# A fixed engine order for the first norm and its products, whole-tile squares, small constants on two other queues, and S5's small steps behind the norm

## The chip, the core and the metric

The kernel runs on one core of a Trainium2 chip. Its engines each work through their own instructions in order: PE (TensorE, matmuls), DVE (VectorE), ACT (ScalarE), POOL (GpSimd) and SP, which here issues DMAs. ACT and POOL can issue DMAs too. The metric is device microseconds (us) of one execution; lower is better.

## The reference

A two-layer trunk on 256 latent and 256 context tokens of 1024 features. Each sub-layer is an RMSNorm, a shift and scale from a conditioning vector (adaLN), the sub-layer itself, and a gated residual. Layer 0 is a half SwiGLU feed-forward of 2816 hidden features, a mixer (latent attention beside an S5 state space), and another half feed-forward. The place of this study is the first feed-forward and what runs beside it:

```python
def rmsnorm(x, g):
    xf = x.astype(jnp.float32)
    y = xf * lax.rsqrt(jnp.mean(xf * xf, axis=-1, keepdims=True) + NORM_EPS)
    return (y * g.astype(jnp.float32)).astype(x.dtype)

def adaln_params(cond, w, b):
    m = jax.nn.silu(cond) @ w + b
    return m.reshape(cond.shape[0], 1, N_MOD, D_MODEL)

def ffn_half_step(h, m, k, g, w_gate, w_up, w_down):
    shift, scale, gate = m[:, :, 3 * k], m[:, :, 3 * k + 1], m[:, :, 3 * k + 2]
    hn = modulate(rmsnorm(h, g), shift, scale)
    return h + 0.5 * gate * swiglu(hn, w_gate, w_up, w_down)

def s5_discretise(lam_re, lam_im, log_step, b_re, b_im):
    ...
    step = jnp.exp(log_step.astype(f32))[:, None]
    a_bar = jnp.exp(lam * step)
    b = lax.complex(b_re.astype(f32), b_im.astype(f32))
    b_bar = ((a_bar - 1.0) / lam)[..., None] * b
    return a_bar, b_bar
```

## The kernel before, in words

**Data.** The activations `res` lie transposed in SBUF, 128 features by 8 tiles by 512 tokens (context first). Weights come in 512 KB blocks of 128 x 1024. A product in fp32 is made of three matmuls of high and low parts, wh·xh, wh·xl and wl·xh (L160 to L162 in `mm3`); the high part of a weight block is a cast on ACT (L150), the low part a subtraction on DVE (L151), both in `wload`. There are four buffers for blocks as loaded (`raw`), four for blocks as split (`w`), and six PSUM banks (`mm`) for products, two more (`ps`) for other things.

**Start (`build`).** SP loads `res`, the conditioning vectors `ct`, S5's parameters, then the first layer's first two modulation vectors' weights `modw0` in sixteen blocks of 512 KB with the first four feed-forward blocks between them, and the small constants `sel`, `ident`, `modb`, `gain`, `sig` behind the first two blocks. The squares for the norm are taken for each tile and each half of the tokens (ACT) and summed on DVE (L297, L298).

**First norm and its products (`norm_proj` with `lead`).** `mod_first(i)` makes shift and scale of tile i: eight matmuls (L191), a copy (L200), two products with `sel` (L203), and small fixes on DVE (`mod_fix`, L177 to L182). `rstd_steps` takes the mean of squares by PE (L255) and the reciprocal root on DVE in three iterations (L266 to L275), `rstd_rows` spreads it over the partitions (L284). `norm_tile` makes tile i's normed input: L315 on DVE, the high part on ACT (L320), the low part on DVE (L322). Four weight blocks are multiplied tile by tile into four banks; I call this the lead.

**Then the feed-forward (`ffn`).** The hidden features come in three chunks of 6, 8 and 8 blocks. For every block: silu (L470), times up (L471), split (L166, L167). After a chunk, `down` makes eight products of 18 (later 24) matmuls, and each leaves its bank through `residual` (L435), which multiplies by the gate. Beside this run background jobs, moved on by `tick` at given rates: S5's preparation (`s5_prepare` with `s5_small`, 128x64 steps on DVE, then `s5_chunk`) and the other modulation vectors (`mod_job`): each is eight 512 KB loads into two buffers `m` and sixteen reduces on DVE (L227). The gate of the first feed-forward, mod(0,2), is the first vector of `mod_job`.

**Order.** A scheduler lays out each engine's order when the program is built, from the order in which the code is written, from priorities (`high_priority`) and from its estimate of when each input is ready; on the chip each engine then runs its list as it stands.

Of the kernel before, what the change touches and what calls it, by code (L numbers as in the profile page):

```python
# [13 lines left out]
ALU = mybir.AluOpType  # L14
# [50 lines left out]

class Builder:
# [180 lines left out]
    def rstd_steps(self, accs, inv, more=None):  # L247
# [17 lines left out]
        def steps():  # L265
# [5 lines left out]
            for _ in range(3):  # L271
                for c in cs:
# [33 lines left out]
    def norm_tile(self, l, k, i, h, x, keep=True):  # L306
# [14 lines left out]
        return lambda: self.keep(  # L321
            nc.vector.scalar_tensor_tensor(x[:, 1, c0:c1], y, b, x[:, 0, c0:c1], op0=ALU.add, op1=ALU.subtract)  # L322
        )

    def norm_proj(self, l, k, halves, srcs, lead=None, spare=None):
# [4 lines left out]
        if lead is not None:  # L330
            ws = self.w0
            first = self.tc.high_priority
            pss = [self.pm() for _ in srcs]
            with first(offset=SOON):
                mods = [lead(i) for i in range(KT)]
                st = self.rstd_stats([self.acc[h] for h in halves], self.inv_d)
                next(mods[0])
                rb = self.rstd_rows(*st)
                for h in halves:
                    self.rb[h] = rb[:, h[0] : h[1]]  # L340
            for i in range(KT):
                with first(offset=SOON):
                    if i + 1 < KT:
                        next(mods[i + 1])
                    next(mods[i], None)
                    for low in [self.norm_tile(l, k, i, h, xs[i]) for h in halves]:
                        low()
                for w, ps in zip(ws, pss):
                    self.mm3(ps, self.wparts(w, KT)[i : i + 1], self.parts(xs[i : i + 1], 0, T2), i == 0, i == KT - 1)
# [40 lines left out]
        return xs, pss  # L390

# [159 lines left out]
    def s5_small(self):  # L551
# [7 lines left out]
        nc.sync.dma_start(bank[1][:, 0:3, :], t["s5_par"])  # L559
# [24 lines left out]
        expm1(step, lst)  # L584
# [61 lines left out]
        yield  # L646
# [489 lines left out]
    def lru_decay(self):  # L1136
# [6 lines left out]
        v.scalar_tensor_tensor(z, lam, -1.0, lam, op0=ALU.mult, op1=ALU.min)  # L1143
# [216 lines left out]
    def build(self):  # L1360
# [220 lines left out]
```

## Time and profile before

| | us |
|---|---|
| runs, three | 1765.08, 1766.74, 1766.30 |
| median | 1766.3 |
| the profiled execution | 1764.04 |
| its span | 1762.0 |
| PE busy | 1702.8 (97%) |
| DVE busy | 1267.6 (72%) |
| ACT busy | 693.7 (39%) |

The profile is of one execution, whose time is 2.0 us more than the span from its first to its last instruction. A busy share over the whole span hides what happens in a stretch; the change touches the first 130 us, and the rows below are from there, with one place near 1520 us that shows PE behind an idle. In the timeline each row is the start, the time, the engine, the line, the operation, output and inputs, and a count; a bracket tells how long the engine was idle before and what ended that.

### The profile page before, as it was taken

To read this page: it belongs to the slowest core of one execution; us is meant where nothing else is said; L and a number is where in the kernel's file an instruction comes from. 1 tells how busy PE (TensorE), PEld (TensorE's weight loads), DVE (VectorE), ACT (ScalarE), POOL (GpSimd) and SP (SyncE) were. 2 spreads that over 40 slices of the span, in tenths; PEclk is the share of its full clock that TensorE was granted. 3 is DMA by queue.
4 is the path that set the end of the run, shared out by engine and by line. 5 is a ranking of instruction groups with operands and counts; after the bars stand their busy time and mean duration, and the time that the engine had idled before them with its cause. 6 is when DMAs were issued, how large, how long until landed. Compare 5 with 4: busy or idle time off the path is not lost.

```text
span 1762.0 us, 24867 instructions
## 1 busy us (share of the span) xinstructions
PE 1702.8 (97%) x9380; PEld 1443.5 (82%) x9380; DVE 1267.6 (72%) x2545; ACT 693.7 (39%) x1101; POOL 13.2 (1%) x47
## 2 busy tenths in 40 slices
PE   5999999999989999999999999999999999699998
PEld 3788878889878788778888888888888888499998
DVE  7999999987488668776676686555543576976675
ACT  4433333443445654222222233222222357554443
POOL 0000000000000000000000000000000000000000
PEclk9999999999998999999999999999999999899999
DMA  9566767662465453564554443555533225155552
GB/s 330 172 221 213 228 212 229 215 189 95 126 188 166 132 188 107 171 216 147 164 190 157 159 141 124 181 185 155 169 120 96 96 96 187 67 171 189 183 183 90
DMA packets 107480, 292.65 MB, mean 166 GB/s; under 512 B 21152, under 2 KB 35360, under 8 KB 107104
## 3 DMA queue, kind: packets, MB, share of 16 engines
q1 hardware_dynamic: 101504, 286.86, 50.6%
q10 hardware_dynamic: 5216, 2.62, 0.8%
q0 software_dynamic: 640, 1.57, 0.3%
q8 instruction: 74, 1.21, 0.3%
q14 instruction: 46, 0.38, 0.1%
HBM read 272.20 MB, written 18.28 MB: 165 GB/s over the span
## 4 chain that ended last, share of the span: by engine, by line
PE 89%; DVE 6%; DMA 2%; issue 1%; SPq 1%; ACT 1%; DVEq 0%; ACTq 0%
PE mm L160 25%; PE mm L162 25%; PE mm L161 25%; PE mm L157 7%; DVE w L151 1%; DMA h<-in_modw_dram 1%; PE mm L1207 1%; SPq L1040 1%; DMA x<-d_g 1%; PE mm L907 1%; DVE x L322 0%; DVE nt L315 0%; PE mm L191 0%; PE ps L690 0%; PE ps L1118 0%
## 5 line engine op out<-in xcount | busy, mean ns | idle before, releaser
L150 ACT CAST w<-raw 128x1024 fp32r<-128x1024 f32 (+2 forms) x324 | 328.8, 1019 | 530.6 <-PE mm L162 262.2
L161 PE MATMUL mm<-x,w 128*128 128x512 f32 (+1 forms) x1424 | 519.8, 365 | 0.0
L162 PE MATMUL mm<-x,w 128*128 128x512 f32 (+1 forms) x1424 | 519.2, 365 | 0.0
L160 PE MATMUL mm<-x,w 128*128 128x512 f32 (+1 forms) x1424 | 514.6, 367 | 3.5 <-ACT x L320 2.2
L151 DVE TENSOR_TENSOR w<-raw,w 128x1024 fp32r<-128x1024 f32 (+2 forms) x324 | 383.8, 1186 | 150.5 <-ACT w L150 149.3
L160 PEld LDWEIGHTS mm<-x,w 128*128 128x128 f32 x1424 | 267.4, 189 | 49.5 <-ACT x L320 2.5
L161 PEld LDWEIGHTS mm<-x,w 128*128 128x128 f32 x1424 | 268.6, 189 | 43.8 <-issue 2.0
L162 PEld LDWEIGHTS mm<-x,w 128*128 128x128 f32 x1424 | 268.5, 189 | 43.9 <-issue 1.2
L227 DVE CUSTOM_DVE_ANT_0 junk<-m,sc 128x1024 f32<-128x1024 f32 x224 | 273.0, 1219 | 1.8 <-DMA m<-in_modw_dram 0.4
L160 PE MATMUL mm<-h,w 128*128 128x512 f32 x456 | 178.3, 394 | 0.0
L162 PE MATMUL mm<-h,w 128*128 128x512 f32 x456 | 176.9, 390 | 0.0
L161 PE MATMUL mm<-h,w 128*128 128x512 f32 x456 | 176.7, 390 | 0.0
L435 DVE SCALAR_TENSOR_TENSOR res<-mm,mraw,res 128x256 f32<-128x256 f32 x192 | 86.0, 479 | 96.5 <-PE mm L162 87.2
L471 DVE TENSOR_TENSOR h<-h,mm 128x512 f32<-128x512 f32 x66 | 45.3, 686 | 108.1 <-PE mm L162 95.8
L470 ACT ACTIVATE h<-mm 128x512 f32<-128x512 f32 x66 | 39.5, 598 | 196.0 <-PE mm L162 185.2
L160 PEld LDWEIGHTS mm<-h,w 128*128 128x128 f32 x456 | 85.6, 188 | 18.9 <-issue 1.1
L162 PEld LDWEIGHTS mm<-h,w 128*128 128x128 f32 x456 | 85.6, 188 | 18.5 <-issue 0.6
L161 PEld LDWEIGHTS mm<-h,w 128*128 128x128 f32 x456 | 85.6, 188 | 18.4 <-issue 1.0
L160 PE MATMUL mm<-hy,w 128*128 128x258 f32 x352 | 99.2, 284 | 0.7 <-DVE g L499 0.7
L162 PE MATMUL mm<-hy,w 128*128 128x258 f32 x352 | 99.6, 283 | 0.0
L161 PE MATMUL mm<-hy,w 128*128 128x258 f32 x352 | 99.6, 283 | 0.0
L157 PE MATMUL mm<-x,w 128*128 128x256 f32 x384 | 66.3, 290 | 6.7 <-DVE x L322 6.2
(371 smaller groups left out, 2002.1 us busy)
## 6 DMA issues: line engine op xcount, KB each, us to landing
raw<-in_wgu_dram SPq DMA_DIRECT2D x176, 512.0 KB, 3.9
m<-in_modw_dram SPq DMA_DIRECT2D x130, 512.0 KB, 4.3
raw<-in_wd_dram SPq DMA_DIRECT2D x64, 512.0 KB, 3.6
raw<-in_wd_dram SPq DMA_DIRECT2D x32, 384.0 KB, 3.3
raw<-in_od_in_dram SPq DMA_DIRECT2D x20, 512.0 KB, 3.5
h<-in_modw_dram SPq DMA_DIRECT2D x12, 512.0 KB, 10.0
raw<-in_ev_in_dram SPq DMA_DIRECT2D x10, 512.0 KB, 3.5
d_mb<-mbt SPq DMA_DIRECT2D x16, 256.0 KB, 3.4
```

What stands on the lines that cost most here:

```text
L150: nc.scalar.copy(hi[:, :n], raw[:, :n])
L151: nc.vector.tensor_sub(lo[:, :n], raw[:, :n], hi[:, :n])
L157: mm = lambda *a, **k: self.keep(self.nc.tensor.matmul(*a, **k))
L160: mm(ps, lhsT=wh, rhs=xh, start=first and i == 0, stop=False)
L161: mm(ps, lhsT=wh, rhs=xl, start=False, stop=False)
L162: r = mm(ps, lhsT=wl, rhs=xh, start=False, stop=last and i == n - 1)
L227: nc.vector.tensor_tensor_reduce(self.junk, w, self.sc[:, v, :], 1.0, 0.0, ALU.mult, ALU.add, raw[:, dt, v : v + 1])
L435: self.nc.vector.scalar_tensor_tensor(r, ps[:, c0:c1], gate[:, i, VEC[h] : VEC[h] + 1], r, op0=ALU.mult, op1=ALU.add)
L470: nc.scalar.activation(s[:, 0, lo:hi], pg[:, lo:hi], AF.Silu)
L471: nc.vector.tensor_mul(s[:, 1, lo:hi], s[:, 0, lo:hi], pu[:, lo:hi])
L907: nc.tensor.matmul(ps, lhsT=q[0:96, c : c + P], rhs=k[0:96, :nk], start=True, stop=True)
L1040: nc.sync.dma_start(uy[g * 16 : (g + 1) * 16, 1, :].rearrange("p (s n) -> p s n", s=L), d_y[i * 8 + g].rearrange("s c n -> c s n"))
```

## The change

1. PE, DVE and ACT instructions of the first norm and its four products are tied, each to the one before it on its engine, so that the scheduler keeps the order in which `lead_products` is written. Its order: modulation of tile 0, statistics, two weight casts, root, rows, norm of tile 0 with the two low weight parts between; then for each tile the four products, with the next tile's norm behind the first product and the modulation of the tile after that ahead of the fourth. In the listing of the changed kernel these instructions all stand at L74, the wrapper's call.
2. The squares are taken of whole tiles of 128x512, into buffers of S5 that are not yet in use; the last tile's squares are added by PE. The root's iterations work on 128x4 at once.
3. `ct`, `modb` and `gain` are loaded by ACT's queue, `sel`, `ident`, `sig` and S5's parameters by POOL's.
4. S5's first exponential and `lru_decay`'s first step are put behind the lead's last low part; S5's small part yields eight times at its end instead of once.

```diff
+class InOrder:
...
+    def __getattr__(self, name):
+        def call(*a, **k):
+            ins = getattr(self.eng, name)(*a, **k)
+            if self.last is not None:
+                dep = mybir.DependencyInfo(mybir.DependencyClass.NoSync, mybir.DependencyReason.DATA)
+                self.tc.add_manual_dep(ins.ins, self.last, dep, reason="in order")
+            self.last = ins.ins.name
+            return ins
...
+                if n == 4:
+                    k(dv.tensor_mul(a, y, y))
+                    k(dv.tensor_mul(a, a, v))
+                    k(dv.scalar_tensor_tensor(y, a, 1.5, y, op0=ALU.add, op1=ALU.mult))
...
+    def lead_products(self, l, k, halves, xs, pss, mods):
...
+        next(mods[0])
+        rb, y = self.rstd_stats(*self.first_sums)
+        ws = [cast(r) for r in self.w0[:2]]
+        next(mods[0], None)
+        rb = self.rstd_rows(rb, y)
...
+        lows = norm(0)
+        ws[0][1]()
+        for low in lows:
+            low()
+        ws[1][1]()
+        next(mods[1])
+        ws += [cast(r) for r in self.w0[2:]]
+        for i in range(KT):
+            product(0, i)
+            if i + 1 < KT:
+                next(mods[i + 1], None)
+                lows = norm(i + 1)
+                if i == 0:
+                    ws[2][1]()
+                for low in lows:
+                    low()
+                if i == 0:
+                    ws[3][1]()
+            product(1, i)
+            product(2, i)
+            if i + 2 < KT:
+                next(mods[i + 2])
+            product(3, i)
...
-        nc.sync.dma_start(bank[1][:, 0:3, :], t["s5_par"])
+        nc.gpsimd.dma_start(bank[1][:, 0:3, :], t["s5_par"])
...
-        expm1(step, lst)
+        with self.tc.issue_after(self.last_low.ins):
+            expm1(step, lst)
...
-        yield
+        for _ in range(8):
+            yield
...
+            sq = [self.slot("mb", [P, T2]), self.slot("mbt", [P, T2]), et[:, 0], et[:, 1]]
+            acc = self.slot("bank", [P, 912])[:, :T2]
             for i in range(KT):
-                for h in both:
-                    self.stat(i, h)
+                A.activation(sq[i % 4] if i else acc, self.res[:, i], AF.Square)
+                if 0 < i < KT - 1:
+                    V.tensor_add(acc, acc, sq[i % 4])
+            self.first_sums = [acc], self.inv_d, sq[(KT - 1) % 4]
```

In the changed kernel the lines move: the weight's low part is L180, products L189 to L191, reduces L256, the eviction L508, S5's small matmuls L785.

**The order on PE at the start.** Before (mm_68 to mm_71 are the four products' banks, mm_77 and mm_79 the modulation of tiles 0 and 1):

```order
L191 MATMUL mm_77_332<-h_21_175,ct_18_127 32x256 x4
L191 MATMUL mm_77_332<-h_22_176,ct_18_127 32x256 x4
L255 MATMUL ps_73_297<-inv_d_169,acc_44_236 128x1 x2
L255 MATMUL ps_73_297<-inv_d_169,acc_45_238 128x1 x2
L203 MATMUL mm_77_332<-sel_179,nt_78_341 128x2 x2
L191 MATMUL mm_79_347<-h_27_199,ct_18_127 32x256 x4
L191 MATMUL mm_79_347<-h_28_200,ct_18_127 32x256 x4
L203 MATMUL mm_79_347<-sel_179,nt_80_356 128x2 x2
L284 MATMUL ps_72_296<-ident_181,rs_y_75_303 128x128 x4
L160 MATMUL mm_68_292<-x_60_284,w_24_191 128x512
```

and now (mm_52 and mm_53 are the first two of the four products' banks, mm_56 and mm_67 the modulation of tiles 0 and 1, bank and et the sums of squares):

```order
L74 MATMUL mm_56_256<-h_21_184,ct_18_127 32x256 x4
L74 MATMUL mm_56_256<-h_22_185,ct_18_127 32x256 x4
L74 MATMUL ps_59_268<-inv_d_133,bank_43_227 128x1
L74 MATMUL ps_59_268<-inv_d_133,et_40_224 128x1
...
L74 MATMUL ps_59_268<-inv_d_133,et_40_224 128x1
L74 MATMUL mm_56_256<-sel_139,nt_57_265 128x2 x2
L74 MATMUL ps_58_267<-ident_141,rs_y_61_278 128x128 x4
L74 MATMUL mm_67_315<-h_25_192,ct_18_127 32x256 x4
L74 MATMUL mm_67_315<-h_26_193,ct_18_127 32x256 x4
L74 MATMUL mm_52_252<-x_44_244,w_63_292 128x512 x3
L74 MATMUL mm_67_315<-sel_139,nt_68_324 128x2 x2
L74 MATMUL mm_53_253<-x_44_244,w_64_294 128x512 x3
```

The statistics matmuls are twice as many, the rows (`ident`) have moved ahead of the modulation of tile 1, and each weight block's three matmuls now stand together.

**The order on DVE beside the norm.** Before, around the low part of tile 1 (x_61 is its normed input, sb0 and sb1 hold S5's small values):

```order
L322 SCALAR_TENSOR_TENSOR x_61_285<-nt_85_399,mraw0_0_282,x_61_285 128x256
L580 TENSOR_TENSOR sb1_20_163<-sb1_20_163 128x64
L322 SCALAR_TENSOR_TENSOR x_61_285<-nt_86_402,mraw0_0_282,x_61_285 128x256
L582 TENSOR_TENSOR sb1_20_163<-sb1_20_163 128x64
L591 TENSOR_TENSOR sb1_20_163<-sb1_20_163 128x64
L604 TENSOR_TENSOR sb0_19_162<-sb1_20_163 128x64
L622 TENSOR_TENSOR s5_rho_726<-sb1_20_163 128x64
L613 TENSOR_TENSOR sb1_20_163<-sb0_19_162,sb1_20_163 128x64
L177 TENSOR_TENSOR mraw0_0_282<-mm_83_383,modb_183 128x2
L177 TENSOR_TENSOR mraw0_1_283<-mm_83_383,modb_183 128x2
L598 TENSOR_TENSOR sb1_20_163<-sb1_20_163 128x64
L616 TENSOR_TENSOR sb0_19_162<-sb0_19_162,sb1_20_163 128x64
```

and now, the last tile's low parts and what stands behind them:

```order
L74 SCALAR_TENSOR_TENSOR x_51_251<-nt_95_556,mraw0_0_242,x_51_251 128x256
L74 SCALAR_TENSOR_TENSOR x_51_251<-nt_96_559,mraw0_0_242,x_51_251 128x256
L640 TENSOR_SCALAR sb1_20_182<-sb1_20_182 128x64
L610 TENSOR_SCALAR sb1_20_182<-sb1_20_182 128x64
L611 TENSOR_SCALAR sb1_20_182<-sb1_20_182 128x64
L615 TENSOR_SCALAR sb1_20_182<-sb1_20_182 128x64
L616 TENSOR_TENSOR sb1_20_182<-sb1_20_182 128x64
L615 TENSOR_SCALAR sb1_20_182<-sb1_20_182 128x64
```

S5's small steps stood among the norm's; now all but five of them follow the last low part, and the first hidden block's L544 among them.

**The order on DVE at the first down product.** Before, from the last of the gate's reduces on (mraw0_2 is the gate mod(0,2); mm_204, mm_211 and so on are the down products' banks; w_241, w_248, w_256 weight blocks):

```order
L227 ISA junk_110_625,mraw0_2_819<-m_148_998,sc_109_624 128x1024
L227 ISA mraw0_2_819 128x1
L730 TENSOR_TENSOR et_177_1193<-et_177_1193,sb0_19_162 128x8x4
L686 TENSOR_TENSOR mb_159_1078<-mb_159_1078,tm_145_979 128x512
L151 TENSOR_TENSOR w_248_1668<-raw_247_1666,w_248_1668 128x768
L177 TENSOR_TENSOR mraw0_2_819<-mraw0_2_819,modb_183 128x16
L701 TENSOR_TENSOR tm_145_979<-pb_114_749,bank_144_977 128x576
L182 TENSOR_SCALAR mraw0_2_819<-mraw0_2_819 128x16
L702 TENSOR_TENSOR gs_162_1090<-gs_162_1090,tm_145_979 128x576
L435 SCALAR_TENSOR_TENSOR res_75<-mm_204_1354,mraw0_2_819,res_75 128x256 x2
L435 SCALAR_TENSOR_TENSOR res_75<-mm_211_1414,mraw0_2_819,res_75 128x256 x2
L435 SCALAR_TENSOR_TENSOR res_75<-mm_219_1466,mraw0_2_819,res_75 128x256 x2
```

and now, from the split of w_247 to the first evictions (mm_182 and mm_189 are the first two down products; the rows left out are seven more of the gate's reduces, each with its second row, and S5's steps):

```order
L180 TENSOR_TENSOR w_247_1711<-raw_246_1709,w_247_1711 128x1024
L256 ISA junk_98_586,mraw0_2_763<-m_108_782,sc_97_585 128x1024
L256 ISA mraw0_2_763 128x1
...
L256 ISA junk_98_586,mraw0_2_763<-m_128_901,sc_97_585 128x1024
L256 ISA mraw0_2_763 128x1
L206 TENSOR_TENSOR mraw0_2_763<-mraw0_2_763,modb_143 128x16
L256 ISA junk_98_586,mraw0_3_1014<-m_142_1015,sc_97_585 128x1024
L256 ISA mraw0_3_1014 128x1
L211 TENSOR_SCALAR mraw0_2_763<-mraw0_2_763 128x16
L508 SCALAR_TENSOR_TENSOR res_75<-mm_182_1268,mraw0_2_763,res_75 128x256 x2
L508 SCALAR_TENSOR_TENSOR res_75<-mm_189_1315,mraw0_2_763,res_75 128x256 x2
```

The gate's reduces had all run ahead of the seventh and eighth down products' weight splits; now nine of sixteen stand behind the split of w_247, a block for the next chunk, and the evictions behind them.

**PE at the same place**, now (mm_220 is the sixth down product, mm_229 the seventh, which takes the bank of mm_182):

```order
L191 MATMUL mm_220_1523<-h_152_1090,w_219_1520 128x512
L189 MATMUL mm_220_1523<-h_172_1209,w_219_1520 128x512
L190 MATMUL mm_220_1523<-h_172_1209,w_219_1520 128x512
L191 MATMUL mm_220_1523<-h_172_1209,w_219_1520 128x512
L785 MATMUL ps_139_983<-gs_137_973,bank_119_860 32x128 x4
L785 MATMUL ps_139_983<-gs_138_978,bank_119_860 32x128 x4
L189 MATMUL mm_229_1574<-h_100_592,w_228_1571 128x512
```

Between the two products PE has only two groups of S5's matmuls.

## Rows read from the trace of the kernel before

**Rows 1.** The page, part 1: busy time, share of the span, instructions.
```profile
PE 1702.8 (97%) x9380; PEld 1443.5 (82%) x9380; DVE 1267.6 (72%) x2545; ACT 693.7 (39%) x1101; POOL 13.2 (1%) x47
```
**Rows 2.** Stretches: length, busy PE, PEld, DVE, ACT, POOL, then clock, DMA share, GB/s.
```profile
28.20:35.00 6.80, 6.80 (x44) 3.62 (x45) 6.66 (x40) 2.06 (x6) 0.00 (x0) 1.00 1.03 411
62.00:126.00 64.00, 63.60 (x296) 51.54 (x297) 61.31 (x120) 24.63 (x39) 0.11 (x1) 1.00 0.63 199
```
**Rows 3.** The timeline of the front: start, time, engine, line, operation.
```profile
14.74 1.87 PE L255 MATMUL ps<-inv_d,acc 128*128 128x1 f32 x8
...
16.64 0.16 DVE L266 TENSOR_SCALAR rs_v<-ps 128x4 f32<-128x4 f32 x1 [0.54 <-PE ps L255]
...
22.52 0.35 DVE L275 SCALAR_TENSOR_TENSOR rs_y<-rs_a,rs_y 128x1 f32<-128x1 f32 x4
...
23.97 2.05 PE L284 MATMUL ps<-ident,rs_y 128*128 128x128 f32 x8
...
25.43 1.22 DVE L151 TENSOR_TENSOR w<-raw,w 128x1024 fp32r<-128x1024 f32 x1
...
26.74 0.86 DVE L315 SCALAR_TENSOR_TENSOR nt<-res,mraw,ps 128x256 f32<-128x256 f32 x2
...
28.20 2.08 PE L160 MATMUL mm<-x,w 128*128 128x512 f32 x4 [2.18 <-ACT x L320]
...
61.11 0.39 PE L162 MATMUL mm<-x,w 128*128 128x512 f32 x1
...
62.19 0.19 PEld L160 LDWEIGHTS mm<-x,w 128*128 128x128 f32 x1 [1.12 <-ACT w L150]
```
**Rows 4.** The timeline of the first down product, the same columns.
```profile
118.44 0.39 PE L162 MATMUL mm<-h,w 128*128 128x512 f32 x1
...
118.60 1.22 DVE L227 CUSTOM_DVE_ANT_0 junk<-m,sc 128x1024 f32<-128x1024 f32 x1
118.67 0.39 PE L160 MATMUL mm<-h,w 128*128 128x512 f32 x1
...
119.74 0.08 DVE L227 DVE_READ_ACCUMULATOR2_ANT mraw<- 128x1 f32 x1
...
125.57 3.22 DVE L435 SCALAR_TENSOR_TENSOR res<-mm,mraw,res 128x256 f32<-128x256 f32 x8
...
134.68 1.05 ACT L150 CAST w<-raw 128x1024 fp32r<-128x1024 f32 x1 [3.63 <-PE mm L162]
```
**Rows 5.** The chain of waits from 0 to 90 us: start, time, step.
```profile
35.38 0.34 PE mm L203 x4
...
39.07 1.86 PE mm L191 x32
```
**Rows 6.** DMA issues: queue, count, KB each, median us to landing.
```profile
m<-in_modw_dram SPq DMA_DIRECT2D x130, 512.0 KB, 4.3
...
d_y<-ys POOLq DMA_DIRECT2D x8, 128.0 KB, 2.9
```
**Rows 7.** Groups on DVE, 0 to 58.1 us: busy time, mean ns, idle before.
```profile
L577 DVE TENSOR_TENSOR sb<-sb 128x64 f32<-128x64 f32 x12 | 2.6, 214 | 0.1
```
**Rows 8.** Groups on DVE by shape, 62 to 126 us, the same columns.
```profile
L700 DVE TENSOR_TENSOR gs<-pa,bank 128x576 f32<-128x576 f32 x4 | 2.8, 751 | 0.0
...
L684 DVE TENSOR_TENSOR mb<-pa,bank 128x512 f32<-128x512 f32 x4 | 2.7, 683 | 0.0
...
L730 DVE TENSOR_TENSOR et<-et,sb 128x128 f32<-128x128 f32 x1 | 0.3, 284 | 0.0
```
**Rows 9.** Tile m, 60 to 140 us: its loads, from issue to landing.
```profile
DMA to landing us min/median/max: 3.5/4.2/4.6
```
**Rows 10.** The timeline of PE near 1520 us.
```profile
1520.18 8.86 PE L1311 MATMUL mm<-hy,x 128*128 128x256 f32 x32 [6.24 <-DVE x L1296]
```
**Rows 11.** Stretches behind that idle, columns as in rows 2.
```profile
1520.20:1523.60 3.40, 3.40 (x8) 2.78 (x9) 3.40 (x6) 0.63 (x1) 0.00 (x0) 0.50 0.00 0
1523.60:1526.00 2.40, 2.40 (x12) 2.12 (x12) 2.40 (x5) 0.00 (x0) 0.00 (x0) 1.00 0.00 0
```

More of the change, by code (lines that the diff above doesn't have):

```diff
@@ L63, with __init__, __getattr__ @@
 LN_PARTS = _split3(math.log(2.0), 9, 11)
+class InOrder:
+    def __init__(self, tc, eng):
+        self.tc, self.eng, self.last = tc, eng, None
+    def __getattr__(self, name):
[6 more added lines that the diff above has]
+            return ins
+        return call
+class InOrderCore:
+    def __init__(self, tc, nc):
+        self.nc = nc
+        self.tensor, self.vector, self.scalar = (InOrder(tc, e) for e in (nc.tensor, nc.vector, nc.scalar))
+    def __getattr__(self, name):
+        return getattr(self.nc, name)
 class Builder:
@@ L330, in norm_proj @@
         if lead is not None:
-            ws = self.w0
-            first = self.tc.high_priority
             pss = [self.pm() for _ in srcs]
[L334 to L349, printed above, removed]
+            with self.tc.high_priority(offset=SOON):
+                self.nc = self.core
+                self.lead_products(l, k, halves, xs, pss, [lead(i) for i in range(KT)])
+                self.nc = self.tc.nc
             return xs, pss
@@ L390, in norm_proj, with cast, norm, product @@
         return xs, pss
+    def lead_products(self, l, k, halves, xs, pss, mods):
+        nc = self.nc
+        def cast(raw):
+            w = self.wp.tile([P, 2, 1024], F32R, tag="w", name=self.uid("w"))
+            nc.scalar.copy(w[:, 0], raw)
+            return w, lambda: nc.vector.tensor_sub(w[:, 1], raw, w[:, 0])
+        def norm(i):
+            return [self.norm_tile(l, k, i, h, xs[i]) for h in halves]
+        def product(b, i):
+            w = ws[b][0]
+            self.mm3(pss[b], self.wparts((w[:, 0], w[:, 1]), KT)[i : i + 1], self.parts(xs[i : i + 1], 0, T2), i == 0, i == KT - 1)
+        next(mods[0])
[3 more added lines that the diff above has]
+        rb = self.rstd_rows(rb, y)
+        for h in halves:
+            self.rb[h] = rb[:, h[0] : h[1]]
+        lows = norm(0)
[21 more added lines that the diff above has]
+            product(3, i)
     def parts(self, xs, c0, c1):
@@ L1380, in build @@
         self.inv_d, self.inv_q, self.inv_kv = invs
-        small = lambda: [
-            setattr(self, nm, self.const(shape, nm, t[nm]))
-            for nm, shape in (("sel", [P, 2]), ("ident", [P, P]), ("modb", [P, 2, 9, KT]), ("gain", [P, 7, KT]), ("sig", [P, 3]))
-        ]
+        for nm, shape, q in (
+            ("sel", [P, 2], nc.gpsimd),
+            ("ident", [P, P], nc.gpsimd),
+            ("modb", [P, 2, 9, KT], nc.scalar),
+            ("gain", [P, 7, KT], nc.scalar),
+            ("sig", [P, 3], nc.gpsimd),
+        ):
+            setattr(self, nm, self.const(shape, nm, t[nm], queue=q))
+        s5 = self.s5_prepare()
+        next(s5)
         self.mw0, self.w0 = [], []
```

34 lines of the change are left out of this document (20 added, 14 removed).

## The prediction

> **What bounds the kernel now.** I read the page first, then the stretches, then the front and the first down product in the timeline. TensorE is busy 97% of the span [rows 1], and from 62 to 126 us for 63.60 of 64.00 us; DVE is busy for 61.31 of the same 64, and for 6.66 of 6.80 us where the products begin [rows 2]. So PE sets the time, and behind it DVE has hardly a gap for the first 130 us: work put later on DVE comes out later at its end.
>
> The front, in order [rows 3]: the eight statistics matmuls take 1.87 us from 14.74, the rsqrt chain on DVE runs from 16.64 to 22.87 (22.52 + 0.35), the rows are spread by PE from 23.97, a weight's low part is taken at 25.43, the first norm at 26.74, the first product begins at 28.20. The lead's last matmul starts at 61.11 (and PE is free of it near 61.35); the next weight load stands 1.12 us idle and comes at 62.19.
>
> The second place is the first down product. Its result leaves PSUM only through L435, which wants the gate mod(0,2); this comes out of sixteen reduces on DVE, each 1.22 us long, 1.14 from its start to the next instruction (118.60 to 119.74) [rows 4]. The gate was done just ahead of 125.57, where eight evictions run in 3.22 us; the sixth down product's weight buffer came free at 134.68, where ACT casts the next block into it [rows 4]. Six banks hold six down products; the seventh needs the first one's bank. In this run that bank was free some 8 us before PE wanted it: 134.68 against 125.57 + 0.8 for the first bank's two evictions (3.22 / 8 x 2). That margin is what this change is about.
>
> **The change part by part.** *The front.* Whole-tile squares whose last tile PE adds make sixteen statistics matmuls of eight: +1.87, at the same price. The rsqrt chain of 6.23 us had splits and S5 rows among its own; in program order it is 3 steps and 3 times 3 dependent instructions on 128x4, 12 in all. A row of this kind lasts 0.16 [rows 3]; with the hand-over between dependent ones I take 0.24, between 0.16 and 0.35 (the last step before): 2.9, so -3.3. The rows no longer stand behind tile 1's modulation matmuls: 23.97 against 22.87, -1.1. No split stands between rows and first norm: 25.43 to 26.65, of which 0.7 lay beside the rows' matmuls, so about -0.7 (bounds 0 and -1.2). Tile 1's modulation matmuls now stand ahead of the first product: +0.7 (0.93 a tile, half of 1.86 [rows 5], less what lies beside the norm). First loads are issued a little earlier: -1 (0 to -1.5). Sum: 1.87 - 3.3 - 1.1 - 0.7 + 0.7 - 1 = -3.5, first product at about 24.7.
>
> Half of that is given back. All four low parts were taken before the first product or just at it; now two of them, and the norm of tile 1, stand inside the first round. From the first norm on, about 23.4, DVE owes four splits at 1.13 (1.22 less what laps over), two tiles of norm and low parts at 0.86 a pair [rows 3] and small fixes: 4.5 + 3.4 + 0.6 = 8.5, so the fourth product of tile 0 ends near 32. Behind it PE owes 28 products of three matmuls, 84 x 0.23 (118.44 to 118.67 [rows 4]) = 19.2, five tiles' modulations at 0.93, six times L203 at 0.34 [rows 5], and about 1.9 for changes of form and a late load: 27.8. The lead ends near 59.7, where it ended at 61.35: -1.7; the pause behind it shrinks by 0.5. **Front: -2.2**, bounds 0 (all given back) and -5.
>
> *Constants on other queues.* They are issued sooner and land in a few us: POOL's transfers landed in 2.9 us, the modulation blocks on SP in 4.3 [rows 6]. I take nothing beyond the 1 us above. The Trainium skill, "SBUF - State Buffer" (the warning on the "DVE blocks DMA" trap in its part on the two sides of SBUF), speaks against POOL's queue: its descriptors are written by GpSimd, which certain DVE instructions lock out. No row here shows such a lock: POOL's eight transfers of one kind landed in 2.9 us, within 1.5 us of SP's. What it would do is the third rival.
>
> *S5 behind the last low part.* Some 140 small S5 rows of 128x64 ran among the norm's before; a row lasts 0.21 [rows 7], 0.13 from start to start. Now all but five come after the lead: 140 x 0.13 = 18 us of DVE, moved from a stretch where PE waited for DVE little to one where DVE is full. In the order, the gate's reduces stand behind them: only one of the sixteen stands ahead of the sixth down product's weight split, and between the split of w_247 and the second eviction of mm_182 stand eleven reduces (nine of the gate, two of mod(0,3)). This split is the trap: w_247 goes into the buffer of w_219, the sixth down product's weights, so its cast waits until PE has finished that product. PE then wants the seventh, mm_229, whose bank is mm_182's. So PE stands, from the end of the sixth down product, for:
> cast 1.05 [rows 4]; split 1.13; eleven reduces x 1.14 = 12.5; nineteen S5 and gate rows between them, two of 128x576 at 0.75, one of 128x512 at 0.68, six of 128x128 at 0.28 [rows 8], ten smaller at a mean of 0.28, 6.7 in durations, less 0.08 each for lapping = 5.2; two evictions 0.8. Together 20.7. The modulation blocks have two buffers; a block lands 3.5 to 4.6 us after issue [rows 9], and two reduces with the rows beside them fill about 3.1, so three blocks come 0.5 to 1.4 late: +2. Signals between engines +0.5. **Stall: 23** (21 to 27).
>
> PE comes out of it at half clock. Behind a 6.24 us idle, ended at 1520.18 [rows 10], the granted clock was 0.50 for the 3.4 us to 1523.6, then 1.00 [rows 11]: level 1.2 instead of 2.4 GHz, so half of 3.4 is lost: **+1.7**.
>
> *Is any of it hidden or won back?* PE is the bound, so a stall of PE is time unless later work of PE is waiting on something else. S5's transposes that PE had done by then before are now done later: the same work, neither sum changes. DVE stays 12 to 18 us of work behind and loses no slack it needs, since later evictions do not wait for a modulation: 0, bounds -3 and +5.
>
> Sum: -2.2 + 23 + 1.7 = +22.5 on the profiled execution's 1764.0 (span 1762.0 and 2.0 around it) = 1786.5. The median of the three runs, 1766.3, is 2.3 above the profiled one: 1788.8, **1789 us**.
>
> **The rivals.** *Short stall (1770 to 1781).* DVE, which takes its rows in order, is ahead of what I count: if w_247's cast gets its buffer sooner or reduces overlap the wait, only part of the eleven stands in PE's way. For it: DVE's rows ahead of w_247 have some waits that I could only sum. Against: the buffer chain above is fixed by the order. +4 to +15. Chance 0.06.
>
> *No stall: the change does what it is written to do (1760 to 1766).* The gate's reduces would have to be done within the 8 us margin; it decides whether S5's rows ahead of the first eviction cost DVE less than 8 us more than before. For it: the front frees DVE of some 3 us. Against: 18 us moved. Then only the front's 0 to -5 is left, 1764 in the middle. This is the faster side. Chance 0.08.
>
> *The constants come late.* By the rule above the transfers of `sel` and `ident` would wait for DVE: the chain that needs them ends on DVE at about 19 to 20, and a landing of 2.9 us from there puts the row matmuls 3 to 4 us later, eats the front's gain and leaves the stall: 1789 + 3 = 1792, up to 1794. For it: DVE is full there. Against: DVE waits for the statistics just before (0.54 [rows 3]), and the transfers are issued before DVE's first sum. Chance 0.04.
>
> *DVE stays the bound through the first feed-forward (1797 to 1816).* After the stall DVE has the same backlog; if silu products and splits are then late chunk after chunk, another 10 to 25 us come on top. For it: DVE's 61.31 of 64.00. Against: PE was busy 63.60 of the same 64 [rows 2], so a full DVE alone did not hold it. Chance 0.05.
>
> *The order does nothing:* front as before, no stall, 1765 to 1769. Chance 0.02.
>
> **How the numbers follow.** Forecast 0.75 (1782 to 1797 by its own bounds), the others 0.06, 0.08, 0.04, 0.05, 0.02. The range 1779 to 1798 holds the forecast, late constants, and an edge of the short stall and of the bound DVE: about 0.81. About 0.2%, 3.5 us, is what a measurement of this kernel can tell from no change: faster 0.05 (the larger half of the case without a stall), same 0.06 (the rest of it, the order that does nothing, and a stall of a few us), slower 0.89.
>
> **What would show it.** One idle of 20 to 27 us on PE near 130 us, ahead of mm_229's first matmul, ended by the eviction L508; clock 0.50 behind it; eleven L256 reduces inside; the first product at 24 to 25.5 and the lead's end at 59 to 61. If that idle is under 15 us, or PE's idle comes elsewhere, the step on the gate's place is wrong; if the first product starts later than 28, the front is.

## The result, and the profile after

The changed kernel took 1788.87 us (median of 4 runs, 1788.55 to 1789.97), the kernel before beside it 1765.69 (4 runs): 1.0135 of it, 95% interval 1.0122 to 1.0148, 23.2 us slower. The span of the profiled execution grew from 1762.0 to 1786.8.

The page of the changed kernel, part 1, to be held beside [rows 1]: PE and DVE are as busy as before in microseconds, so nearly all of the 24.8 us is waiting.

```profile
PE 1704.7 (95%) x9388; PEld 1444.8 (81%) x9388; DVE 1271.4 (71%) x2492; ACT 692.6 (39%) x1092; POOL 15.4 (1%) x51
```

What PE waited for in its first 200 us, in the changed kernel (total, times, longest):

```profile
PE mm L189 <- DVE res L508: 21.6, 1, 21.6
...
PE ps L785 <- DVE gs L777: 1.5, 1, 1.5
...
PE mm L74 <- DVE w L74: 1.3, 1, 1.3
```

One wait of 21.6 us on an eviction. The timeline of the changed kernel around it, DVE, ACT and PE together (compare [rows 4]):

```profile
130.35 1.04 ACT L179 CAST w<-raw 128x1024 fp32r<-128x1024 f32 x1 [1.46 <-PE mm L191]
...
132.01 1.22 DVE L180 TENSOR_TENSOR w<-raw,w 128x1024 fp32r<-128x1024 f32 x1
132.15 0.43 PE L785 MATMUL ps<-gs,bank 128*32 128x128 f32 x8 [1.48 <-DVE gs L777]
...
133.15 1.22 DVE L256 CUSTOM_DVE_ANT_0 junk<-m,sc 128x1024 f32<-128x1024 f32 x1
...
135.24 1.23 DVE L256 CUSTOM_DVE_ANT_0 junk<-m,sc 128x1024 f32<-128x1024 f32 x1 [0.69 <-DMA m<-in_modw_dram]
...
140.77 1.23 DVE L256 CUSTOM_DVE_ANT_0 junk<-m,sc 128x1024 f32<-128x1024 f32 x1 [0.92 <-DMA m<-in_modw_dram]
...
147.05 1.23 DVE L256 CUSTOM_DVE_ANT_0 junk<-m,sc 128x1024 f32<-128x1024 f32 x1 [0.24 <-DMA m<-in_modw_dram]
...
151.80 0.17 DVE L211 TENSOR_SCALAR mraw<-mraw 128x16 f32<-128x16 f32 x1
...
153.22 3.22 DVE L508 SCALAR_TENSOR_TENSOR res<-mm,mraw,res 128x256 f32<-128x256 f32 x8
...
154.15 0.80 PE L189 MATMUL mm<-h,w 128*128 128x512 f32 x1 [21.57 <-DVE res L508]
```

Read it from the bottom. PE's seventh down product starts at 154.15, when the first bank has been evicted (L508 at 153.22, the gate's last step L211 at 151.80). Above stands the split at 132.01: its cast at 130.35 came when PE had finished the sixth down product. Between split and eviction DVE runs without a gap but for 0.69, 0.92 and 0.24 us on modulation blocks. The eviction of [rows 4] at 125.57 is now 27.65 us later.

The clock behind it, stretches of the changed kernel, columns as in rows 2:

```profile
154.10:157.20 3.10, 3.06 (x7) 2.50 (x8) 3.10 (x9) 0.00 (x0) 0.00 (x0) 0.50 0.55 194
157.20:160.00 2.80, 2.80 (x13) 2.26 (x13) 2.80 (x8) 0.00 (x1) 0.00 (x0) 0.99 0.00 0
```

Seven matmuls at the lower level, 0.43 apart where 0.23 is usual: 7 x 0.20 = 1.4 us.

And the front, timeline of the changed kernel (compare [rows 3]):

```profile
17.70 0.16 DVE L74 TENSOR_SCALAR rs_v<-ps 128x4 f32<-128x4 f32 x1 [5.67 <-PE ps L74]
...
19.74 0.16 DVE L74 SCALAR_TENSOR_TENSOR rs_y<-rs_a,rs_y 128x4 f32<-128x4 f32 x1
...
19.96 2.08 PE L74 MATMUL ps<-ident,rs_y 128*128 128x128 f32 x8 [1.45 <-DVE rs_y L74]
21.97 1.94 PE L74 MATMUL mm<-h,ct 128*32 128x256 f32 x16
22.07 0.87 DVE L74 SCALAR_TENSOR_TENSOR nt<-res,mraw,ps 128x256 f32<-128x256 f32 x2 [1.80 <-PE ps L74]
...
23.83 0.62 PE L74 MATMUL mm<-x,w 128*128 128x512 f32 x1
...
25.86 1.42 PE L74 MATMUL mm<-x,w 128*128 128x512 f32 x5
...
28.62 0.50 PE L74 MATMUL mm<-x,w 128*128 128x512 f32 x1 [1.35 <-DVE w L74]
...
60.57 0.50 PE L189 MATMUL mm<-x,w 128*128 128x512 f32 x1
```

The root takes 2.2 us (17.70 to 19.90) instead of 6.23, and the first product starts at 23.83 instead of 28.20. Part of that goes back in the first round, where the third product waits 1.35 us for its weight's low part. The first product behind the lead starts at 60.57, where it was 62.19: 1.6 us are left of 4.4.

**The tally.** I compare the start of the same weight cast on ACT in both traces: the fifth (the first behind the lead), the 85th (early in the mixer), the 89th (behind the mixer's attention). The changed kernel stands at -1.6 (59.48 against 61.10), +23.5 (524.60 against 501.07) and +25.0 us (643.09 against 618.07). So: front -1.6, the two waits of PE 21.6 + 1.5, the clock 1.4, in sum +22.9 of the 23.5; another 1.5 in the mixer.

### The profile page after: what moved, and what is told of

It is laid out like the page before. It is cut to its first block, busy times and chain, and to the rows that moved or that the text cites. A ratio compares the mean times of both kernels' runs of the same rounds, so it can differ in the third digit from the quotient of the medians.

```text
span 1786.8 us, 24832 instructions
## 1 busy us (share of the span) xinstructions
PE 1704.7 (95%) x9388; PEld 1444.8 (81%) x9388; DVE 1271.4 (71%) x2492; ACT 692.6 (39%) x1092; POOL 15.4 (1%) x51
## 4 chain that ended last, share of the span: by engine, by line
PE 88%; DVE 6%; DMA 3%; ACT 1%; SPq 1%; issue 1%; DVEq 0%; ACTq 0%
PE mm L190 25%; PE mm L191 25%; PE mm L189 25%; PE mm L186 6%; PE mm L982 1%; DVE w L180 1%; DMA h<-in_modw_dram 1%; SPq L1115 1%; PE mm L74 1%; PE mm L1283 1%; DMA sc<-in_modw_dram 1%; PE mm L1034 1%; DVE junk L256 1%; DMA m<-in_modw_dram 1%; DVE x L359 0%
## 5 line engine op out<-in xcount | busy, mean ns | idle before, releaser
L179 ACT CAST w<-raw 128x1024 fp32r<-128x1024 f32 (+1 forms) x320 | 324.8, 1019 | 505.6 <-PE mm L191 244.6
L189 PE MATMUL mm<-x,w 128*128 128x512 f32 (+1 forms) x1392 | 505.2, 366 | 6.7 <-ACT x L195 6.5
L191 PE MATMUL mm<-x,w 128*128 128x512 f32 (+1 forms) x1392 | 508.5, 366 | 0.0
L190 PE MATMUL mm<-x,w 128*128 128x512 f32 (+1 forms) x1392 | 508.2, 365 | 0.0
L180 DVE TENSOR_TENSOR w<-raw,w 128x1024 fp32r<-128x1024 f32 (+1 forms) x320 | 378.7, 1185 | 153.1 <-ACT w L179 147.8
L189 PEld LDWEIGHTS mm<-x,w 128*128 128x128 f32 x1392 | 262.0, 189 | 49.9 <-ACT x L195 7.3
L190 PEld LDWEIGHTS mm<-x,w 128*128 128x128 f32 x1392 | 263.6, 189 | 43.1 <-issue 2.2
L191 PEld LDWEIGHTS mm<-x,w 128*128 128x128 f32 x1392 | 263.6, 189 | 42.1 <-issue 1.0
L256 DVE CUSTOM_DVE_ANT_0 junk<-m,sc 128x1024 f32<-128x1024 f32 x224 | 272.9, 1218 | 3.7 <-DMA m<-in_modw_dram 2.2
L189 PE MATMUL mm<-h,w 128*128 128x512 f32 x456 | 179.1, 395 | 21.6 <-DVE res L508 21.6
L191 PE MATMUL mm<-h,w 128*128 128x512 f32 x456 | 177.6, 391 | 0.0
L508 DVE SCALAR_TENSOR_TENSOR res<-mm,mraw,res 128x256 f32<-128x256 f32 x192 | 85.4, 478 | 94.6 <-PE mm L191 85.9
L189 PEld LDWEIGHTS mm<-h,w 128*128 128x128 f32 x456 | 86.0, 189 | 40.6 <-DVE res L508 21.8
L544 DVE TENSOR_TENSOR h<-h,mm 128x512 f32<-128x512 f32 x66 | 45.2, 685 | 103.0 <-PE mm L191 96.1
L191 PEld LDWEIGHTS mm<-h,w 128*128 128x128 f32 x456 | 85.9, 188 | 17.8
L191 PE MATMUL mm<-hy,w 128*128 128x258 f32 x352 | 99.6, 283 | 0.0
L189 PE MATMUL mm<-hy,w 128*128 128x258 f32 x352 | 99.2, 283 | 0.0
```

What stands on the lines that cost most here:

```text
L179: nc.scalar.copy(hi[:, :n], raw[:, :n])
L180: nc.vector.tensor_sub(lo[:, :n], raw[:, :n], hi[:, :n])
L189: mm(ps, lhsT=wh, rhs=xh, start=first and i == 0, stop=False)
L190: mm(ps, lhsT=wh, rhs=xl, start=False, stop=False)
L191: r = mm(ps, lhsT=wl, rhs=xh, start=False, stop=last and i == n - 1)
L256: nc.vector.tensor_tensor_reduce(self.junk, w, self.sc[:, v, :], 1.0, 0.0, ALU.mult, ALU.add, raw[:, dt, v : v + 1])
```

## The experiments

My theory: S5's 18 us, moved behind the lead, push the gate's reduces back behind a split that itself waits for PE. Rivals: the fixed order or the queues cost the time; or S5 late is a loss wherever the gate stands.

The table gives, for every run, the median against its own runs of before, the distance of the three casts from before in the profiled execution, and its span (us). The casts and the span are those of one execution, the median is that of all. A time is usually some 2 us over its span; with S5 on POOL the median is 8.7 over the profiled span (its four times run from 1775.58 to 1783.19, and the first was profiled), so its casts hold for that time alone.

| run | median | ratio, 95% interval | 5th | 85th | 89th | span |
|---|---|---|---|---|---|---|
| the change | 1788.87 | 1.0135 (1.0122 to 1.0148) | -1.6 | +23.5 | +25.0 | 1786.8 |
| S5 early again | 1772.09 | 1.0044 (1.0026 to 1.0062) | +4.6 | +5.1 | +8.3 | 1771.6 |
| S5 late alone | 1792.93 | 1.0159 (1.0142 to 1.0176) | +0.3 | +27.2 | +27.1 | 1789.4 |
| S5 behind the gate | 1800.11 | 1.0191 (1.0175 to 1.0206) | -0.7 | +29.8 | +37.9 | 1799.6 |
| S5 behind tile 3 | 1784.16 | 1.0122 (1.0093 to 1.0150) | +0.3 | +16.4 | +18.1 | 1780.4 |
| S5 on POOL | 1782.47 | 1.0083 (1.0063 to 1.0103) | +8.9 | +8.9 | +10.7 | 1773.8 |
| S5 behind tile 0 | 1776.14 | 1.0056 (1.0034 to 1.0079) | +3.0 | +6.1 | +15.6 | 1778.5 |
| parts 2 and 3 alone | 1773.27 | 1.0041 (1.0026 to 1.0056) | -1.1 | -0.6 | +8.7 | 1771.6 |
| S5 on POOL, else before | 1769.88 | 1.0023 (1.0014 to 1.0033) | +4.7 | +4.7 | +4.9 | 1767.7 |
| squares alone | 1772.22 | 1.0034 (1.0022 to 1.0047) | -1.0 | -1.0 | +6.0 | 1768.4 |
| queues alone | 1766.98 | 1.0006 (0.9997 to 1.0015) | -0.8 | +0.6 | +4.5 | 1767.7 |
| fewer reduces | 1782.59 | 1.0097 (1.0081 to 1.0112) | -2.1 | +11.7 | +19.8 | 1781.4 |
| filled wait | 1784.04 | 1.0112 (1.0095 to 1.0129) | -1.0 | -0.5 | +18.9 | 1782.2 |

**S5 early again.**

```diff
-        with self.tc.issue_after(self.last_low.ins):
-            expm1(step, lst)
+        expm1(step, lst)
...
-        for _ in range(8):
-            yield
+        yield
```

> The changed kernel with its part 4 undone: S5's small steps and the decay's first step are no longer put behind the lead's last low part, and S5's small part yields once. In the order all sixteen of the gate's reduces stand ahead of the seventh down product's weight split again, and 118 of 127 counted S5 rows stand ahead of the last low part. Theory (the gate comes late because S5's 18 us moved in front of its reduces): no idle of PE over 3 us between 120 and 160 us, and the time falls by 21 to 26 us against the changed kernel, to 1762 to 1768. Rival (the fixed order of the front or the queues are themselves the loss, and S5's place matters little): the time stays over 1780.

The idle is gone: this run's stretch around it has PE busy throughout.

```profile
120.00:160.00 40.00, 40.00 (x192) 32.33 (x191) 37.95 (x74) 14.48 (x22) 0.11 (x1) 1.00 0.70 223
```

The time fell by 16.8, not by 21 to 26, and the median lies 4 above the range. What is left is mostly the lead, which ends 4.6 us later than before and 6.2 later than the changed kernel's (4.6 + 1.6); another 3.2 came in the mixer (+5.1 to +8.3). The lead's start in PE's timeline of this run:

```profile
24.85 0.80 PE L74 MATMUL mm<-x,w 128*128 128x512 f32 x1
...
27.83 2.48 PE L74 MATMUL mm<-x,w 128*128 128x512 f32 x5
30.89 0.80 PE L74 MATMUL mm<-x,w 128*128 128x512 f32 x1 [0.57 <-DVE w L74]
...
33.48 2.93 PE L74 MATMUL mm<-x,w 128*128 128x512 f32 x6
```

Five matmuls in 2.48 us stand some 0.43 apart, the spacing of the stretch granted 0.50 above; in the changed kernel the same five took 1.42 from 25.86, at most 0.26 apart, near the 0.23 of the stretch at 1.00. So I take PE to be still at the lower level here, which the changed kernel had left by its second product. This is read from the spacing alone: the profile's clock column prints 1.00 for all of this stretch, as it does for 28.20 to 35.00 in [rows 2], where the first four matmuls also take 2.08 us [rows 3]. Part of the 6.2 is that clock, which did not rise at the same time even for one and the same front: the run with S5 behind the gate has it, takes 2.48 us for the same five matmuls, and stands at -0.7 instead of -1.6. So S5's place in the lead, with the later clock, costs a tied front some 6 us in this execution, and its place behind the lead cost 23.

**S5 late alone**, part 4 on the kernel before:

```diff
-        expm1(step, lst)
+        with self.tc.issue_after(self.last_low.ins):
+            expm1(step, lst)
...
-        yield
+        for _ in range(8):
+            yield
```

> The kernel before with part 4 alone: only S5's small steps are put behind the last low part, with the eight yields; front, squares and queues as before. In the order eleven reduces stand between the twenty-second weight split and the first eviction, as in the changed kernel. Theory: the same idle of PE, 19 to 25 us ahead of the seventh down product, and 1783 to 1792. Rival (the loss needs the fixed order of the front): under 1772. If DVE, freed of S5 in the lead, also makes the front faster, that is worth 0 to 3 us here.

PE's timeline of this run:

```profile
156.66 0.80 PE L160 MATMUL mm<-h,w 128*128 128x512 f32 x1 [22.57 <-DVE res L439]
```

The same idle, without the fixed order, the squares or the queues. At 1792.93 the median is 0.9 above the range. The loss is part 4's, and part 4 alone is enough for it. Part 4 is two edits, the place behind the last low part and the eight yields; no run takes one without the other and leaves S5 behind the whole lead.

**S5 behind tile 3**, a smaller dose:

```diff
+            ins = self.keep(
...
+            if not l and not k and i < 4:
+                self.last_low = ins
```

> The changed kernel, but S5's small steps are put behind tile 3's last low part, not tile 7's: about half of them, 51 of 127 counted, then run within the lead. In the order four reduces instead of eleven stand between the same weight split and the first eviction. Theory (the stall is the sum of what stands in DVE's order there): 1.05 + 1.13 + 4 x 1.14 + ten S5 rows of some 2.8 + 0.8 + 0.5 = an idle of 10 us (8 to 13) at the same product, and 1774 to 1780. Rival (a stall set by something else, a load or a clock, of fixed size): an idle near 21 us again, or none.

```profile
146.76 0.77 PE L189 MATMUL mm<-h,w 128*128 128x512 f32 x1 [13.38 <-DVE res L510]
```

With four reduces in the way instead of eleven, PE stood 13.4 us instead of the two waits' 23.1: 9.7 went, where seven reduces at 1.14 and S5 rows of 5.2 - 2.8 come to 10.4. I had put the size at 10 (8 to 13), and it lies just over that. In this run's timeline DVE stood 1.5 us there for a transfer of S5's, ahead of a memset, and the split began at 135.75, 2.29 us behind its cast and not 1.05, since one more reduce stood ahead of it. The time is 4 us over the range; the lead ended 1.9 later than the changed kernel's.

**S5 behind the gate.**

```diff
-        self.start(s5, 2.5)
+        def behind_gate():
+            while (0, 2) not in self.mod:
+                yield
+            self.last_low = self.last_fix
+            yield from s5
+
+        self.start(behind_gate(), 2.5)
```

> The changed kernel, but S5's small steps start behind the last step of the gate mod(0,2) and not behind the last low part. All sixteen reduces stand then ahead of the fourth down product's split. Theory: no idle near 130 us, and the front's gain of 2 to 4 us is left: 1760 to 1766, unless S5, now later still, comes late at the end of the first feed-forward (then up to 1772, with PE or ACT waiting near 400 to 425 us). Rival (S5 late is the loss wherever the gate is): over 1780.

The idle at the down product went, and up to the 61st cast the kernel was ahead of before by 6.6 us (349.24 against 355.87). Most of that is work still owed: from 66 us to that cast PE had spent 9.04 us on 103 of S5's matmuls (tile `ps`), where before it had spent 14.34 on 168. Then PE waited, in this run's list for 60 to 480 us:

```profile
PE ps L765 <- DVE et L805: 12.0, 1, 12.0
PE ps L765 <- DVE mb L761: 11.8, 3, 8.6
```

and the clock fell with it (stretches, columns as in rows 2):

```profile
400.00:420.00 20.00, 7.42 (x61) 6.52 (x59) 17.26 (x45) 5.58 (x13) 0.11 (x1) 0.78 0.33 115
420.00:440.00 20.00, 6.88 (x44) 4.54 (x45) 17.23 (x42) 6.77 (x14) 0.33 (x3) 0.50 0.41 136
```

Both my range (1760 to 1766, up to 1772 with a late S5) and its reason fall. S5's work on DVE, put off by the gate's reduces, was not absorbed by what slack DVE had; it came due at the end of the first feed-forward, where S5's transposes must be done: 36 us between the 61st and the 85th cast (from -6.6 to +29.8), 23.8 of them in these two waits, 5.3 S5's matmuls still owed, the rest for the most part at the lower clock. Here the rival was right: S5 late is a loss even with the gate early, only in another place.

**Fewer reduces**, on the kernel just shown:

```diff
+                    if l == 0 and m in (6, 7):
+                        nc.vector.tensor_copy(raw[:, dt, v : v + 1], w[:, :1])
+                        continue
```

> The kernel with S5 behind the gate, without the reduces of layer 0's modulation vectors 6 and 7: they are loaded but a one-column copy stands in place of each of the 32 reduces, so the second feed-forward is computed with other values. It takes 32 x 1.06 = 34 us from DVE in the first feed-forward, and none from PE. Theory (S5's lateness at the end of the first feed-forward is DVE's work put off, no more): the idles of PE at S5's transposes between 400 and 445 us go, 20 us or more of them, and the time falls from 1800 to 1762 to 1775. Rival (S5's chunks are a chain of their own whose length does not hang on DVE's load): the idles stay over 15 us and the time over 1785.

What is left of the two waits, in this run's list for 0 to 700 us:

```profile
PE ps L768 <- DVE mb L764: 5.5, 4, 2.1
PE ps L768 <- DVE et L808: 0.5, 1, 0.5
```

Of 23.8 us 6.0 are left, 3.6 of them between 400 and 445 us, where the theory wanted 20 gone. At the 85th cast the kernel stood at +11.7 instead of +29.8, so some 18 us of S5's lateness were DVE's work put off. The time, 1782.59, misses the range by 8. The distance from before grew from -7.9 at the 40th cast (227.29 against 235.22) to +11.7 at the 85th and +19.8 behind the mixer's attention, though DVE now had slack (busy 25.56 of 40 us from 300 to 340). What held the kernel there, and how much a better order would win, was not tried.

**S5 behind tile 0**, `i < 1` in the edit of the smaller dose, and one yield:

> The changed kernel, with S5's small steps behind tile 0's last low part and one yield: 93 of 127 counted rows run within the lead, none within its first round. No reduce stands between the split that waits for the sixth down product and the first eviction, only two rows. Theory: an idle of PE there of 3 to 4 us (1.05 + 1.13 + 0.3 + 0.8) or none, a lead that ends 1 to 3 us later than the changed kernel's 60.5, and 1763 to 1771. Rival (S5's rows in the lead cost PE as much as in the kernel with part 4 undone, 1772): 1771 to 1776.

```profile
PE mm L189 <- DVE res L510: 3.1, 1, 3.1
```

The wait came out as summed (3 to 4). Up to the mixer the kernel stood at +6.1; the mixer's attention then took 9.4 more, which the expectation did not hold. The median, 1776.14, lies on the rival's side, but it is the middle of two pairs: 1772.27 and 1773.17 us at a mean granted clock of 0.989 and 0.988, 1779.11 and 1780.40 at 0.985 and 0.984, and the profile is of the last. So neither the theory's range nor the rival's reason is shown.

**S5 on POOL**, on the changed kernel without part 4, and on the kernel before:

```diff
-        e = nc.vector
+        e = nc.gpsimd
```

> The changed kernel with S5's small steps on POOL (all but the one reciprocal), from the start and not behind the last low part, one yield at their end. DVE then has none of the 18 us, neither in the lead nor behind it, and all sixteen reduces stand ahead of the seventh down product's split. Theory (the loss is DVE's 18 us wherever they stand ahead of the gate, or late at S5's tail): neither the idle near 130 us nor one near 400 to 425 us, and the front's gain stays: 1758 to 1764. Rival (POOL's steps are too slow, over 0.4 us a row, so that S5's first chunk waits for them on DVE, in whose order splits and evictions stand behind it): an idle of PE near 60 to 100 us and over 1770.

> The kernel before with S5's small steps on POOL, all but the reciprocal. It takes 18 us of DVE out of the first 60 us. Theory (PE is the bound there, DVE's rows stand in its way only at the first round): 0 to 4 us faster than before, 1761 to 1765. Rival (POOL's rows are slow or hold DVE up where both read SBUF): slower than 1766, with S5's first chunk late.

No idle at the down product in either, but the lead ends 9 and 5 us later. A 128x64 row takes POOL longer than the 0.21 us of [rows 7]: from 0.34 (L577 again, in the run on the kernel before) to 0.62 in its costliest groups of such rows (groups on POOL, the first of the run on the changed kernel, the second of that on the kernel before):

```profile
L713 POOL TENSOR_TENSOR sb<-pb,sb 128x64 f32<-128x64 f32 x8 | 5.0, 624 | 0.6
```
```profile
L643 POOL TENSOR_TENSOR sb<-pa,sb 128x64 f32<-128x64 f32 x8 | 4.8, 603 | 0.6
```

and the one reciprocal left on DVE waits for it, with the norm's tiles queued behind (DVE's waits, 20 to 70 us, of the run on the changed kernel; PE's next product then waited 5.0 us, up to 47.18, for a normed tile):

```profile
DVE sb L684 <- POOL sb L683: 6.5, 1, 6.5
```

That is the change's own fault once more, one instruction at the head of a full queue. The rival was right in both on the time and on POOL's slow rows, but not on the place: the loss is in the lead, and from 60 to 100 us PE waited only 1.4 and 1.9 us in all, none of it for S5.

**Parts 2 and 3 alone**, and each by itself:

```diff
+            acc = self.slot("bank", [P, 912])[:, :T2]
             for i in range(KT):
-                for h in both:
-                    self.stat(i, h)
+                A.activation(sq[i % 4] if i else acc, self.res[:, i], AF.Square)
+                if 0 < i < KT - 1:
+                    V.tensor_add(acc, acc, sq[i % 4])
...
-            self.nc.sync.dma_start(tl, src)
+            (queue or self.nc.sync).dma_start(tl, src)
```

> The kernel before with parts 2 and 3 alone: whole-tile squares with PE's added tile, the root on 128x4, small constants on ACT's and POOL's queues; no ties, S5 as before. Theory (the gain of the front comes from these, and S5 stays early enough): the first product 1 to 3 us earlier than 28.20 and 1762 to 1766, no idle near 130 us. Rival (the ties carry the front, or the constants land late on the other queues): 1766 to 1770, the first product at 28 or later.

> The kernel before with part 2 alone: squares of whole tiles, the last added by PE, the root on 128x4. All reduces stand ahead of the seventh down product's split. Theory: the root's chain shrinks by 2 to 3 us, the doubled statistics matmuls take 1.9 back: the first product 0 to 2 us earlier, 1763 to 1767. The mixer's stretch of 104 us from the eighty-eighth weight cast, which took 9 us more where parts 2 and 3 stood together, says whether that comes with the squares. Rival: S5's buffers, taken by the sums, start S5's rows late: an idle near 130 us, over 1770.

> The kernel before with part 3 alone: ct, modb and gain on ACT's queue, sel, ident, sig and S5's parameters on POOL's. Theory: the first modulation blocks are issued earlier, the first product 0 to 1.5 us earlier: 1763 to 1767, if the mixer's stretch stays near 104 us. Rival (POOL's transfers wait for DVE, or ACT's issues hold up its squares): the first product later than 28.2 and over 1767.

At the fifth cast they stand at -1.1, -1.0 and -0.8, at the 85th at -0.6, -1.0 and +0.6: each part alone gives the front about 1 us and the two together no more, and PE waited for no small constant from POOL's queue. None came out faster: in the profiled executions the mixer's attention took 9.3, 7.0 and 3.9 us more. For parts 2 and 3 the stretch from the 88th to the 89th cast shows what these are, the kernel before first:

```profile
513.78:618.07 104.29, 94.80 (x588) 75.15 (x587) 78.64 (x155) 59.15 (x136) 7.43 (x20) 0.92 0.52 155
```
```profile
513.16:626.77 113.61, 99.82 (x588) 78.60 (x587) 79.48 (x155) 59.38 (x136) 7.45 (x20) 0.88 0.49 147
```

Both have 588 matmuls there; they kept PE busy 5.0 us longer at a granted clock of 0.88 instead of 0.92, and PE was idle 4.3 us longer, which are waits for a split on ACT (L166; PE's waits from 505 to 645 us, the kernel before first):

```profile
PE mm L160 <- ACT x L166: 0.4, 1, 0.4
```
```profile
PE mm L160 <- ACT x L166: 6.1, 2, 3.8
```

So the loss is half clock and half waiting, and not the clock alone. Queues alone, on the other hand, lost in its profiled execution what not all of its runs lost: five of its eleven runs had a mean granted clock of 0.985 and took 1767.08 to 1769.82 us, the profiled one among them; the other six had 0.988 to 0.990 and took 1763.02 to 1766.98.

PE's groups of matmuls come in the same order there in the changed kernel and with parts 2 and 3, and both stand 6.9 us at the same transposes; but the stretch at the lower clock around the end of that wait is 6.8 us long in the one and 20.4 in the other, the changed kernel first:

```profile
549.80:556.60 6.80, 3.35 (x17) 3.38 (x17) 6.74 (x15) 4.70 (x13) 0.00 (x0) 0.50 0.71 216
```
```profile
528.00:548.40 20.40, 18.48 (x71) 15.98 (x72) 13.19 (x31) 9.53 (x24) 1.00 (x3) 0.50 0.48 151
```

The kernel before had 17 us at 0.50 there too, behind an idle of 7.4 us, so this length is not what sets parts 2 and 3 off from it; a second stretch at 0.50, from 609.8 to 616.6, the kernel before did not have.

**Filled wait**, parts 2 and 3 with four matmuls ahead of the first transposes:

```diff
+                if self.warm:
+                    for _ in range(self.warm):
+                        self.keep(nc.tensor.matmul(ps, lhsT=self.ident, rhs=self.res[:, 0, :], start=True, stop=True))
+                    self.warm = 0
```

> Parts 2 and 3 on the kernel before, as in the run that took 1773, and four matmuls of 128x512 that nobody reads, ahead of the first head's transposes in the mixer, where PE stood 6.9 us and then ran at half clock for 20.5 us. They also move S5's matmuls of that place ahead of the transposes. Theory (the front's 1.4 us gained up to the mixer are lost again there to the clock alone): the granted clock stays at 1.00 or is 0.50 for under 10 us behind that place, the stretch of 113.6 us from the eighty-eighth weight cast falls to 104 to 108, and the time to 1763 to 1768. Rival (the stretch is long by its order of instructions): 111 us or more and over 1770.

```profile
529.48 0.66 PE L1036 MATMUL ps<-x,x 128*128 128x64 f32 x2 [7.14 <-DMA x<-d_v]
...
556.36 4.13 PE L947 MATMUL mm<-res,ident 128*128 128x512 f32 x6
```

The test missed its aim. The added matmuls ran at 556, behind the wait and not in it, and PE stood for S5's transfers first, as it did in the kernel before. The stretch came out at 123.7 us and the time at 1784, past the rival's bounds, but in an order of its own. That the loss was the clock's alone, as the theory had it, does not fit the two stretches shown above. Whether a filled wait would keep the clock up stays open.

No version here beats the kernel before. The nearest is the one with the queues alone, which cannot be told from it.

## Why the prediction was right, point by point

- **The stall.** Put at 23 (21 to 27); the two waits are 21.6 + 1.5 = 23.1, at the place named, ended by the eviction named. Of its terms: from the split at 132.01 to the first eviction at 153.22 are 21.2 us, against 1.13 + 12.5 + 5.2 + 2 = 20.8, with eleven reduces and nineteen other rows in it as counted. Late modulation blocks: 1.85 against 2. The 0.5 for signals was taken from no row; what the trace has is 1.66 from the cast's start to the split's, against 1.05 for the cast, and 0.93 from the eviction's start to PE's, against 0.8.
- **The clock.** Put at 1.7 from one idle of 6.24 us; measured 1.4. The lower level was there for seven matmuls.
- **The front.** Put at -2.2 (0 to -5); measured -1.6. The root took 2.2 instead of the 2.9 I took and the first product came at 23.83, 0.9 earlier than forecast and just outside the 24 to 25.5 named as a sign; but tile 1's modulation matmuls took 1.94 there, where I had counted 0.7 at the price of a later tile (1.07 for the sixteen from 29.06), and the lead ended at 60.5, not 59.7. The sum priced every matmul of the lead at 0.23 and had no term for when the clock rises, though the four from 28.20 before take 2.08 us [rows 3]. With the same order but the later rise, the run with S5 behind the gate gained 0.7 and not 1.6. That is more than the miss of 0.6, so that the front came this close is in part luck.
- **Late constants (a rival, 0.04).** The statistics began at once behind the modulation matmuls, and `sel` and `ident` were there when wanted: the rows waited for the root (1.45), not for a transfer. `sel` and `ident` landed 5.9 and 6.2 us after their issue at 1.4 and 2.0, not 2.9 as in [rows 6], but SP's queue had taken 9.1 and 8.5 for them in the kernel before. No delay that would need a lock showed; whether a part of the 5.9 was one, no run tells.
- **DVE "loses no slack it needs".** In the changed kernel it held: from 160 to 500 us PE waited 2.1 us in all. But the reason given does not carry it in general. The stall itself gave DVE 21 us in which PE asked for nothing; without it, in the run with S5 behind the gate, the debt came due at S5's transposes, 36 us by the casts. The prediction did not see that second place, and its number did not need it because the gate's place is paid first.
- **The mixer** I had at nothing; it gave +1.5 in the change, and up to +9.4 in other runs that left its code alone.

Sum: -2.2 + 23 + 1.7 = 22.5 forecast, 23.2 measured between medians.

## What to carry to other kernels

Work moved out of one engine's busy stretch is paid where it lands: ask what stands behind it in that engine's queue, and which of those rows gives a buffer or a bank back to the engine that sets the time. A row that waits (here a split, for the very product before the one that is stuck) turns everything queued behind it into idle time of the other engine. And in the one run that moved it once more, behind the gate, with DVE busy for 36.21 of 40 us from 300 to 340, that only moved the bill.

## What the runs showed that I had not expected

The same order of PE's groups of matmuls behind the same idle of 6.9 us had the lower clock for 6.8 us in one kernel and 20.4 in another. Executions of one program differ too, as queues alone shows (0.985 in five runs, 0.988 to 0.990 in six). Edits of the first 60 us that gained 1 us there lost 4 to 9 in the mixer of the profiled execution, 460 us later; with parts 2 and 3 half of it was waiting. Why the clock stays low so differently was not settled.
